# A two-layer decoder trunk on one core: MLP in a fixed order, weight sums by adding DMAs, norm gains and positions broadcast by TensorE

## The chip, the cores and the metric

The kernel runs on one core of a Trainium2 chip. The metric is the device time of one execution in microseconds. A core has a matrix engine (TensorE, PE in the profile, with its weight loads as PEld), a vector engine (VectorE, DVE), a scalar engine (ScalarE, ACT), GpSimd (POOL) and SyncE (SP), which here only starts DMAs. Each engine works through its own queue in order; semaphores order the engines among each other. TensorE writes to eight PSUM banks of 128 x 512 float32, and all other tiles lie in SBUF.

## What is computed

Two layers, sequence 512, model width 1024, everything in float32. The parts that matter here:

```python
for layer in range(DEPTH):                      # 2
    h = rms_norm(x, g_mix[layer])
    qkv = h @ w_in[layer]                       # 1024 x 3072, three head groups
    ...                                         # three kinds of attention, partial RoPE by positions
    x = x + mix @ w_out[layer]
    h2 = rms_norm(x, g_ffn[layer])
    u = h2 @ w_up[layer]                        # 1024 x 5632
    u = causal depthwise conv(u, width 3) + conv_b
    gate, val = split(u, 2)                     # 2 x 2816
    x = x + (silu(gate) * val) @ w_down[layer]  # 2816 x 1024
return rms_norm(x, g_final)
```

## The kernel before, in words

**Products.** Each float32 operand is split into a part that TensorE's fast float32 format holds (`whi`, a cast on ACT) and the rest (`wlo`, a subtraction on DVE); a product is three matmuls (hi x hi, hi x lo, lo x hi). The splits of the weights run through the whole program: SP loads a raw weight tile of 128 x 1024 (`raw`, five buffers), ACT casts it, DVE subtracts, TensorE uses the pair. The pairs have four buffers (`HL_BUFS`), so a split can start when the unit four before it has been used. One list of "units" gives their order; `use` takes the next units and splits some ahead (line 284).

**Opening.** x is loaded as four row tiles of two halves. For each tile ACT squares x (`square`, line 511), GpSimd multiplies x by the gain `gbc`, a tile of 128 x 512 that a DMA with step 0 fills with the same row in each partition (`load_g`, line 350), and DVE scales the product by the reciprocal root (`norm`, line 533); only the second half of the first tile is done by one DVE operation on x, `rstd` and `gbc`. TensorE transposes the result (`hT_of`, tiles `htp` and `hTh`, `hTl`), and the first projection (`qka`) starts with what is there. The positions come as a tile of 128 x 512 in the same way, on GpSimd's DMA queue (`rope_features`, line 425).

**MLP.** The up-projection runs in blocks: one block is 128 columns of `w_up`, 24 matmuls of 512 columns into one bank, gate (`upg`) and value (`upv`) in turn; f counts the pairs, 22 in all. A block's bank is read by the convolution (ACT scales it, DVE adds two shifted copies: `cg`, `cv`), then SiLU and the product of both on DVE.

The down-projection of f = 0 to 17 isn't done plainly. Three folds of six f take two rows of f (a pair: `g0`, `g1`) times a 2 x 2 block of `w_down` with seven products in place of eight (Winograd's form of Strassen's multiplication). It needs sums of the activations (`s`, on GpSimd, split into `ga` and `gs`) and sums of the weight blocks (`tt`, and one half of `raw`, on GpSimd too): four sums of 128 x 512 per pair.

```python
G.tensor_tensor(out=tt[:, 1], in0=r1[:, 1], in1=r0[:, 1], op=OP.subtract)
G.tensor_tensor(out=r0[:, 1], in0=r0[:, 1], in1=r0[:, 0], op=OP.subtract)
G.tensor_tensor(out=tt[:, 0], in0=r1[:, 1], in1=r0[:, 1], op=OP.subtract)
```

A product is six matmuls of 512 columns; a fold of three pairs has 21 products into four pairs of banks (`dx`, `dy`, `dz`, `dw`). When the first 12 are done, the banks are added up into x (`dc`, `du`, `dv`, `dt`), and the other nine go on in `dx`, `dw`, `dz`. The banks of `upg`, `dx` and `dy` share one set of four, and `upv`, `dz` and `dw` the other: a fold's banks are those of the last up-blocks. f = 18 to 21 are done plainly (`dn`).

**What sets the order.** The opening keeps program order on the engines. In the MLP a list scheduler sets the order of each queue by its own estimates and by priorities: weight splits have priority 300, and the convolutions of the pair before a fold (`held`, line 1073), which is needed only after the fold, have 400.

Of the kernel before, what the change touches and what calls it, by code (L numbers as in the profile page):

```python
# [18 lines left out]
NT = S // 128  # L19
# [13 lines left out]
HOLD_PRIO = 400  # L33
# [30 lines left out]
def kernel(  # L64
# [57 lines left out]
    SIDE = {"sc", "ptp", "pv", "ov", "stk", "htp", "cvp", "upv", "dz", "dw"}  # L122
# [54 lines left out]
    for l in range(DEPTH):  # L177
# [15 lines left out]
        for f0, n in FOLDS:  # L193
            add_up(l, f0 + 2, n)
            for f in range(f0, f0 + n, 2):
                units.append(("s1", w_down, l, f, None))
            for f in range(f0, f0 + n, 2):
                units.append(("s2", w_down, l, f, None))
# [6 lines left out]
    RAWS = {"t": 1, "f": 1, "s1": 2, "s2": 0}  # L205
    SLOTS = {"t": 1, "f": 1, "s1": 2, "s2": 2}
# [4 lines left out]
    def emit_dma(force=False):  # L211
# [15 lines left out]
        elif kind == "f":  # L227
            raw = raw_tile((128, KD, 128))
            nc.sync.dma_start(out=raw, in_=w[l, :, a:a + 128].rearrange("(k p) c -> p k c", p=128))
        elif kind == "s1":  # L230
            raw = [raw_tile() for _ in range(2)]
            for r, k in zip(raw, (a, a + 1)):
                nc.sync.dma_start(out=r, in_=w[l, k * 128:(k + 1) * 128, :].rearrange("p (c n) -> p c n", c=2))
# [6 lines left out]
            raw = r0, r1, tt  # L240
        else:
            raw = None
        raws[u] = raw
        return True

# [8 lines left out]
    def emit_split():  # L254
# [8 lines left out]
        with tc.high_priority(PRIO if u > 3 else 0):  # L263
# [6 lines left out]
            elif kind == "s1":  # L270
                r0, r1, tt = raw
                split[u] = hi_lo(r0), hi_lo(tt)
                kept[l, a] = r1, tt
                n_raw[0] -= 1
            else:

                r1, tt = kept.pop((l, a))
                G.tensor_tensor(out=tt[:, 1], in0=r1[:, 0], in1=tt[:, 0], op=OP.subtract)
                split[u] = hi_lo(r1), hi_lo(tt[:, 1:2], n=1)
                n_raw[0] -= 1  # L280
# [3 lines left out]
    def use(n=1, ahead=2):  # L284
# [3 lines left out]
        taken = sum(SLOTS[units[u][0]] for u in range(u0, u0 + n))  # L288
        while n_split[0] < u0 + n:
            emit_split()  # L290
        while n_split[0] < len(units):
            out = taken + sum(SLOTS[units[u][0]] for u in range(u0 + n, n_split[0] + 1))
            if out > (HL_BUFS if units[n_split[0]][0][0] == "s" else max(n, 1 + ahead)):
                break
# [61 lines left out]

    load_x(0)
    load_g(("mix", 0), g_mix[0])
# [14 lines left out]
    V.tensor_copy(identr, ident)  # L373
    eps_t = const.tile([128, 1], F, name="eps_t")
# [46 lines left out]

    cos_f = const.tile([128, 512], F, name="cos_f")
    sin_f = const.tile([128, 512], F, name="sin_f")

    def rope_features():
        pi = page("pos_i", I32)
        s = positions[0]
        nc.gpsimd.dma_start(out=pi, in_=bass.AP(tensor=s.tensor, offset=s.offset, ap=[[0, 128], [1, 512]]))
        ang, k, r = page("ang"), page("k"), page("r")
        V.tensor_copy(k, pi)  # L430
        V.tensor_scalar(out=ang, in0=k, scalar1=ropec[:, 0:1], scalar2=None, op0=OP.mult)
# [101 lines left out]
    def norm(t, g=None):  # L533
        r = rstd_of(t)
        for c in range(2):
            if g is None or c == 0:
# [387 lines left out]
    def mlp(l, nxt):  # L924
        cv = convs[l]

        def conv(banks, f):

            us = []
            for b, j, name in zip(banks, (f, NF + f), ("cg", "cv")):  # L930
                us.append((page(name), b, j))
            for u, b, j in us:
# [268 lines left out]
```

## Time and profile before

| | |
|---|---|
| median of 3 runs | 1271.05 us (1270.91 to 1273.56) |
| the profiled execution | 1272.82 us, its span 1271.0 us |
| TensorE busy | 1216.7 us (96%) |
| VectorE, ScalarE, GpSimd busy | 931.3, 669.6, 405.6 us |
| moved by DMA | 111.22 MB, 88 GB/s over the span |
| first matmul | 9.56 us after the start |

A row of the timeline gives the start, the duration, the engine, the operation with its tiles (out<-in), and in brackets the idle time before it with what ended it. Nearly all instructions bear line 99, which is a helper that records them; so they are told apart by the names of their tiles. In a row of groups, "x64: 1209/1226/2314" is the count with the shortest, median and longest time in ns, and "| 28.5, 1582 |" the sum in us and the mean in ns.

### The profile page before, as it was taken

Reading aid. Unit: us, or ns where it says so; the run is one execution under the profiler, and the core shown is the slowest. Engines: PE = TensorE matmul, PEld = TensorE weight load, DVE = VectorE, ACT = ScalarE, POOL = GpSimd, SP = SyncE. Lnnn points to the kernel's source line nnn. Section 1 sums busy time; section 2 is a strip of 40 time slices with the busy share of each in tenths; the row PEclk is TensorE's granted clock in tenths of the full one; section 3 lists DMA queues with packets and bytes.
Section 4 is the critical chain, followed back from the end, with each engine's and each line's share of the span. In section 5 each row is a group of like instructions: output and inputs, shape, how many; then the busy total and the mean of one; then the engine's idle time right before and its main releaser. Section 6 shows DMA issues by size and latency. Waiting matters only on the chain.

```text
span 1271.0 us, 16494 instructions
## 1 busy us (share of the span) xinstructions
PE 1216.7 (96%) x5888; PEld 988.9 (78%) x5888; DVE 931.3 (73%) x1619; ACT 669.6 (53%) x1224; POOL 405.6 (32%) x388
## 2 busy tenths in 40 slices
PE   6999999999989999999999999999999899999996
PEld 5877777789877877887888777787988788788785
DVE  6888878576678678678678677774766876776874
ACT  4766777544434444444457658773544344443444
POOL 3011435131254245154211123441124614525413
PEclk9999999999999999999999999999999999999999
DMA  6321212232314323324313121121332242242221
GB/s 225 103 83 51 67 51 69 68 97 86 100 55 127 101 66 105 115 80 125 99 42 117 51 83 50 67 70 50 117 100 84 83 133 83 67 133 83 67 83 67
DMA packets 142562, 111.22 MB, mean 88 GB/s; under 512 B 5386, under 2 KB 124208, under 8 KB 142480
## 3 DMA queue, kind: packets, MB, share of 16 engines
q1 hardware_dynamic: 142064, 109.47, 28.5%
q8 instruction: 46, 0.75, 0.2%
q0 software_dynamic: 272, 0.44, 0.1%
q14 instruction: 36, 0.29, 0.1%
q10 hardware_dynamic: 144, 0.26, 0.1%
HBM read 108.06 MB, written 2.10 MB: 87 GB/s over the span
## 4 chain that ended last, share of the span: by engine, by line
PE 49%; DVE 28%; POOL 9%; issue 7%; ACT 6%; DMA 2%; SPq 0%; POOLq 0%; ACTq 0%; DVEq 0%
DVE wlo L99 10%; PE upg L99 9%; PE upv L99 8%; PE op L99 7%; DVE cv L99 4%; PE qf L99 4%; POOL s L99 4%; ACT whi L99 3%; DVE p L99 3%; PE qka L99 3%; PE dn L99 3%; PE pv L99 3%; DVE cg L99 2%; PE up L99 2%; PE ptp L99 2%
## 5 line engine op out<-in xcount | busy, mean ns | idle before, releaser
L99 DVE TENSOR_TENSOR wlo<-raw,whi 128x1024 fp32r<-128x1024 f32 x196 | 271.1, 1385 | 112.5 <-ACT whi L99 111.5
L99 ACT CAST whi<-raw 128x1024 fp32r<-128x1024 f32 x196 | 203.9, 1047 | 137.4 <-PE dw L99 31.4
L99 POOL TENSOR_SCALAR p<-p,sm 128x512 f32<-128x512 f32 (+3 forms) x128 | 77.3, 612 | 240.8 <-DVE sm L99 149.5
L99 PE MATMUL upg<-hTh,wlo 128*128 128x512 f32 x320 | 125.0, 391 | 2.4 <-DVE wlo L99 2.4
L99 PE MATMUL upg<-hTh,whi 128*128 128x512 f32 x320 | 124.6, 389 | 0.0
L99 PE MATMUL upg<-hTl,whi 128*128 128x512 f32 x320 | 124.5, 389 | 0.0
L99 PE MATMUL upv<-hTh,whi 128*128 128x512 f32 x320 | 124.5, 389 | 0.0
L99 PE MATMUL upv<-hTl,whi 128*128 128x512 f32 x320 | 124.5, 389 | 0.0
L99 PE MATMUL upv<-hTh,wlo 128*128 128x512 f32 x320 | 124.5, 389 | 0.0
L99 POOL TENSOR_TENSOR hn<-x,gbc 128x512 f32<-128x512 f32 x39 | 53.2, 1375 | 174.9 <-ACT hn L99 168.1
L99 ACT ACTIVATE p<-p,sm 128x512 f32<-128x512 f32 (+3 forms) x160 | 89.2, 559 | 33.5 <-DVE sm L99 32.5
L99 POOL TENSOR_TENSOR s<-cv 128x256 f32<-128x256 f32 x36 | 34.6, 980 | 196.8 <-DVE cv L99 196.8
L99 POOL TENSOR_TENSOR tt<-raw 128x512 f32<-128x512 f32 x36 | 54.6, 1516 | 108.9 <-DMA raw<-in_w_down_dram 107.5
L99 ACT ACTIVATE cg<-cg 128x512 f32<-128x512 f32 x44 | 27.8, 632 | 115.2 <-DVE cg L99 115.0
L99 PEld LDWEIGHTS upg<-hTh,wlo 128*128 128x128 f32 x320 | 60.1, 188 | 16.4 <-DVE wlo L99 4.1
L99 PEld LDWEIGHTS upv<-hTh,wlo 128*128 128x128 f32 x320 | 60.1, 188 | 12.5
L99 PEld LDWEIGHTS upg<-hTl,whi 128*128 128x128 f32 x320 | 60.1, 188 | 12.4
L99 PEld LDWEIGHTS upv<-hTh,whi 128*128 128x128 f32 x320 | 60.1, 188 | 12.4
L99 PEld LDWEIGHTS upv<-hTl,whi 128*128 128x128 f32 x320 | 60.1, 188 | 12.4
L99 PEld LDWEIGHTS upg<-hTh,whi 128*128 128x128 f32 x320 | 60.1, 188 | 12.2
L99 DVE TENSOR_TENSOR wlo<-tt,whi 128x1024 fp32r<-128x1024 f32 (+1 forms) x36 | 49.8, 1382 | 25.1 <-ACT whi L99 24.8
L99 ACT CAST ga<-cv 128x256 fp32r<-128x256 f32 (+1 forms) x36 | 18.1, 514 | 87.9 <-DVE cv L99 87.9
(234 smaller groups left out, 3207.5 us busy)
## 6 DMA issues: line engine op xcount, KB each, us to landing
raw<-in_w_up_dram SPq DMA_DIRECT2D x88, 512.0 KB, 3.8
raw<-in_w_down_dram SPq DMA_DIRECT2D x44, 512.0 KB, 3.5
raw<-in_w_in_dram SPq DMA_DIRECT2D x40, 512.0 KB, 3.7
raw<-in_w_out_dram SPq DMA_DIRECT2D x16, 512.0 KB, 3.5
raw<-in_w_in_dram SPq DMA_DIRECT2D x16, 256.0 KB, 3.0
x<-in_x_dram SPq DMA_DIRECT2D x8, 256.0 KB, 7.1
out_dram<-hn SPq DMA_DIRECT2D x7, 256.0 KB, 2.1
gbc<-in_g_mix_dram SPq DMA_DIRECT2D x4, 256.0 KB, 5.6
```

What stands on the lines that cost most here:

```text
L99: i = f(*a, **k)
```

## The change

**Weight sums.** The units s1 and s2 of a pair become four units w1 to w4, and `FOLD_UNITS` gives their order in a fold. The weight sums are done by DMAs that add what they load to what lies in the tile (`accum_op=OP.add`). They can only be started from GpSimd's queue. `w1` is a load of the pair's first column half followed by one add into its second part; `tt` is loaded by SP and gets one add of 512 KB and one of 256 KB; when `w2` has been split from it, one more add of 256 KB makes `w4` of it. Some signs of the sums change with this, so that each weight sum is an addition.

**Fixed order.** From the third f of a layer's MLP to the end of its up-blocks each engine keeps program order, and the program writes that order out: a block's convolution is issued behind the next block's matmuls (`finish_conv`), splits run three units ahead, and work that can wait is put in a list (`later`) for the next block. In the fold, splits, the additions of the banks and the products stand in a given order; the held pair's operands are made behind the fold. The nine last products are in another order (`dx`, `dw`, `dz` per pair become 2, 4, 3 with the last two turned round).

**Opening.** The gain of layer 0's first norm is loaded as two rows of 1 x 512 from ACT's queue, and TensorE multiplies a column of ones by each row, which leaves the gain in all partitions of two PSUM banks (`over_rows`, tile `gb`). GpSimd's multiplications of the first norm go; DVE does each half in one operation. Positions are broadcast in the same way. The squares of the next tile are issued ahead of the transposes of this one.

```diff
+FOLD_UNITS = [("w1", 0), ("w1", 1), ("w2", 0), ("w2", 1), ("w1", 2), ("w2", 2),
+              ("w3", 0), ("w4", 0), ("w3", 1), ("w4", 1), ("w3", 2), ("w4", 2)]
...
-            r0, r1 = raw
-            tt = sb.tile([128, 2, 512], F, name="tt", tag="qkst", bufs=WIDE)
-            G.tensor_tensor(out=tt[:, 1], in0=r1[:, 1], in1=r0[:, 1], op=OP.subtract)
-            G.tensor_tensor(out=r0[:, 1], in0=r0[:, 1], in1=r0[:, 0], op=OP.subtract)
-            G.tensor_tensor(out=tt[:, 0], in0=r1[:, 1], in1=r0[:, 1], op=OP.subtract)
+            raw = raw_tile()
+            b = quarters(l, a)
+            nc.sync.dma_start(out=raw, in_=b[:, 0 if kind == "w1" else 1])
+            if kind == "w1":
+                adding.append((raw[:, 1], b[:, 0, 0]))
...
+    def add_now(dst, src):
+        tc.keep_in_program_order(nc.gpsimd.dma_start(out=dst, in_=src, accum_op=OP.add))
+
+    def add_loaded():
+        while adding:
+            add_now(*adding.popleft())
+
+    def sum_steps(l, a):
+        b = quarters(l, a)
+        tt = sb.tile([128, 2, 512], F, name="tt", tag="qkst", bufs=WIDE)
+        kept[l, a] = tt
+        tc.keep_in_program_order(nc.sync.dma_start(out=tt, in_=b[:, 0]))
+        return [lambda: add_now(tt, b[:, :, 1]), lambda: add_now(tt[:, 0], b[:, 1, 1])]
...
+            elif kind == "w2":
+                tt = kept[l, a]
+                split[u] = hi_lo(tt)
+                add_now(tt[:, 0], quarters(l, a)[:, 1, 0])
...
+    for c in range(2):
+        nc.scalar.dma_start(out=g_row[c], in_=g_mix[0:1, 512 * c:512 * c + 512])
     load_x(0)
-    load_g(("mix", 0), g_mix[0])
...
+    def over_rows(row):
+        b = bank("gb")
+        T.matmul(b, lhsT=ones, rhs=row, start=True, stop=True)
+        return b
...
+        def block(v, f, extra=None):
+            b = bank("upv" if v else "upg")
+            wh, wl = take()
+            for k in range(KD):
+                ah, al = act_h(k)
+                three_f(b, wh[:, k, :], wl[:, k, :], ah, al, k == 0, k == KD - 1)
+            done = finish_conv()
+            add_loaded()
+            while n_split[0] < min(n_used[0] + 3, len(units)):
+                emit_split()
...
         squares(0)
-        norm(0, gbc["mix", 0])
+        norm(0, gains)
         for n in range(NT):
             wts[n] = use(1, 0)
+            if n + 1 < NT:
+                squares(n + 1)
             hT_of(n)
             if n + 1 < NT:
-                squares(n + 1)
-                norm(n + 1)
+                norm(n + 1, gains)
```

How the queues stand now, at three places. First ACT's queue in the opening (`hn` is the squares' output, `whi` the cast of a weight tile, `hTh` the cast of the transposes), before:

```order
L99 ACT_TABLE_LOAD
L99 ACTIVATE hn,ss<-x_0_64 128x512
L99 ACTIVATE hn,ss<-x_1_65 128x512
L99 ACTIVATE rstd<-rstd,eps_t 128x1
L99 ACTIVATE rstd<-rstd 128x1
L99 CAST whi<-raw 128x1024
L99 CAST hTh<-htp 128x4x128 x2
L99 ACTIVATE hn,ss<-x_0_66 128x512
L99 ACTIVATE hn,ss<-x_1_67 128x512
```

With the change:

```order
L367 DMA g_row<-in_g_mix_dram 1x512 x2
L100 ACT_TABLE_LOAD
L100 ACTIVATE hn,ss<-x_0_64 128x512
L100 ACTIVATE hn,ss<-x_1_65 128x512
L100 ACTIVATE rstd<-rstd,eps_t 128x1
L100 ACTIVATE rstd<-rstd 128x1
L100 CAST whi<-raw 128x1024
L100 ACTIVATE hn,ss<-x_0_66 128x512
L100 ACTIVATE hn,ss<-x_1_67 128x512
L100 CAST hTh<-htp 128x4x128 x2
```

Two DMA starts stand at its head, and the squares of the second tile are ahead of the first `hTh`.

Second DVE's queue in the first fold of layer 0, behind the convolution of the last up-block (`wlo` are the weight splits, `du` and `dv` the additions of the banks, `ga` an operand of the held pair):

```order
L99 TENSOR_TENSOR wlo<-raw,whi 128x1024
L99 TENSOR_TENSOR wlo<-tt,whi 128x1024
L99 TENSOR_TENSOR wlo<-raw,whi 128x1024
L99 TENSOR_TENSOR wlo<-tt,whi 128x512
L99 TENSOR_TENSOR du<-dy,dc 128x512 x2
L99 TENSOR_TENSOR dv<-dw,du 128x512 x2
L99 TENSOR_TENSOR dv<-dz,dv 128x512
L99 TENSOR_TENSOR wlo<-raw,whi 128x1024
L99 TENSOR_TENSOR wlo<-tt,whi 128x512
L99 TENSOR_TENSOR dv<-dz,dv 128x512
L99 TENSOR_TENSOR wlo<-raw,whi 128x1024
L99 TENSOR_TENSOR ga<-cv,ga 128x256
```

With the change, from the same point on:

```order
L100 TENSOR_TENSOR wlo<-tt,whi 128x1024
L100 TENSOR_TENSOR wlo<-raw,whi 128x1024
L100 TENSOR_TENSOR wlo<-tt,whi 128x1024
L100 TENSOR_TENSOR wlo<-raw,whi 128x1024
L100 TENSOR_TENSOR wlo<-tt,whi 128x512
L100 TENSOR_TENSOR du<-dc,dy 128x512 x2
L100 TENSOR_TENSOR dv<-dw,du 128x512 x2
L100 TENSOR_TENSOR dv<-dz,dv 128x512 x2
L100 TENSOR_TENSOR wlo<-raw,whi 128x1024
L100 TENSOR_TENSOR wlo<-tt,whi 128x512
L100 TENSOR_TENSOR wlo<-raw,whi 128x1024
```

Five splits stand ahead of the first addition in place of four, no split parts the last two `dv`, and `ga` is gone from the fold; it stands behind it.

Third GpSimd's queue at the same fold, from activation sums (`s`) to the first use of `du`:

```order
L99 TENSOR_TENSOR s_3465<-cv 128x256
L99 TENSOR_TENSOR s_3466<-cv 128x256
L99 TENSOR_TENSOR s_3465<-s_3465,cv 128x256
L99 TENSOR_TENSOR s_3466<-cv,s_3465 128x256
L99 TENSOR_TENSOR tt<-raw 128x512
L99 TENSOR_TENSOR raw<-raw 128x512
L99 TENSOR_TENSOR tt<-raw 128x512
L99 TENSOR_TENSOR tt<-raw,tt 128x512 x3
L99 TENSOR_TENSOR dt<-du,x_0_68 128x512
```

With the change:

```order
L247 DMA tt<-in_w_down_dram 128x512
L247 DMA raw<-in_w_down_dram 128x512
L247 DMA tt<-in_w_down_dram 128x512
L247 DMA raw<-in_w_down_dram 128x512 x2
L100 TENSOR_TENSOR s_3518<-cv 128x256
L100 TENSOR_TENSOR s_3518<-s_3518,cv 128x256
L100 TENSOR_TENSOR s_3519<-cv 128x256
L100 TENSOR_TENSOR s_3519<-s_3518,cv 128x256
L247 DMA tt<-in_w_down_dram 128x512 x3
L100 TENSOR_TENSOR dt<-du,x_0_68 128x512
```

Where GpSimd added tiles it now starts DMAs, most of them ahead of the activation sums; the three starts ahead of `dt` are the adds that make `w4`.

More of the change, by code (lines that the diff above doesn't have):

```diff
@@ L287, in use @@
         n_used[0] += n
[L288 to L294, printed above, removed]
+        while n_split[0] < min(u0 + max(n, 1 + ahead), len(units)):
             emit_split()
@@ L1000, in product, with take, finish_conv @@
             now[0] += 1.36
-        def fold(pairs):
+        def take():
+            n_used[0] += 1
+            return split.pop(n_used[0] - 1)
+        last, cgs, gates, steps, later = [None], {}, {}, deque(), []
+        def finish_conv():
+            if last[0] is None:
+                return None
+            b, v, f = last[0]
+            last[0] = None
+            u = conv(b, NF * v + f, "cv" if v else "cg")
+            if v:
+                gates[f] = gated(cgs.pop(f), u)
+                return f
+            cgs[f] = u
+            later.insert(0, lambda: act(u, u, AF.Silu))
+            return None
@@ new lines, in block @@
+        def block(v, f, extra=None):
+            b = bank("upv" if v else "upg")
+            wh, wl = take()
+            for k in range(KD):
+                ah, al = act_h(k)
+                three_f(b, wh[:, k, :], wl[:, k, :], ah, al, k == 0, k == KD - 1)
+            now[0] += 5.4
+            done = finish_conv()
+            add_loaded()
+            while n_split[0] < min(n_used[0] + 3, len(units)):
+                emit_split()
+            work = later[:]
+            later.clear()
+            for w in work:
+                w()
+            if done is not None and extra:
+                extra(done)
+            if steps:
+                steps.popleft()()
+            last[0] = (b, v, f)
@@ L1044, in fold @@
             for t in range(2):
                 G.tensor_tensor(out=u4[t], in0=u2[t], in1=X[2 + t][0], op=OP.add)
[L1046 to L1051 removed]
+            p(5, 2)
+            for t in range(2):
+                tt(out=u3[t], in0=bw[t], in1=u2[t], op=OP.add)
@@ L1076, in mlp, with rest @@
-        gh, gl = quad("gh"), quad("gl")
+                tt(out=X[t][1], in0=u2[t], in1=bz[t], op=OP.subtract)
+            if hold is not None:
+                later.append(hold)
+            def rest():
+                for t in range(2):
+                    tt(out=X[2 + t][0], in0=bw[t], in1=u4[t], op=OP.add)
+            later.insert(0, rest)
+        bs = first_group()
+        for f in range(2):
+            cg, cvl = conv(bs[2 * f], f, "cg"), conv(bs[2 * f + 1], NF + f, "cv")
+            act(cg, cg, AF.Silu)
+            gates[f] = gated(cg, cvl)
@@ L1077, in mlp @@
+        while f < NF:
+            for v in range(2):
+                block(v, f, plain)
+            f += 1
+        plain(finish_conv())
+        in_order[0] = False
+        gh, gl = gh[0], gl[0]
         f0, n = PLAIN
-        for j in range(n):
-            g = held[j] if j < 2 else up_pair(f0 + j)
-            A.copy(gh[:, j, :], g)
-            V.tensor_tensor(out=gl[:, j, :], in0=g, in1=gh[:, j, :], op=OP.subtract)
         def act_g(k):
```

299 lines of the change are left out of this document (172 added, 127 removed).

## The prediction

> **What bounds the kernel now.** I read the page's busy shares first, then the busy time by stretch, then what TensorE waited for, then the order of time at two places.
>
> ```profile
> PE 1216.7 (96%) x5888; PEld 988.9 (78%) x5888; DVE 931.3 (73%) x1619; ACT 669.6 (53%) x1224; POOL 405.6 (32%) x388
> PE   6999999999989999999999999999999899999996
> 408.69 5.44 PE upv L99 x24
> ```
>
> TensorE is busy 96% of the span, so what can be won is its idle time plus the time in which it runs slowly after a pause. The forty slices place it: the first slice, the last, and two that read 8. The third row, from the chain, gives the rate where nothing is in the way: 24 matmuls of 512 columns in 5.44 us, 0.2267 us each. A fold of three pairs has 3 x 7 x 6 = 126 of them, so it needs 28.56 us; the twelve up-blocks between two folds need 65.28 us. Against that stands the table by stretches, cut where TensorE's first matmul of each fold and its first up matmul behind it start (columns: stretch, length, TensorE busy, clock, DMA share, GB/s):
>
> ```profile
> 302.28:367.56 65.28, 65.28 (x290) 1.00 0.30 89
> 367.56:402.20 34.64, 31.06 (x128) 0.95 0.27 76
> 402.20:468.36 66.16, 65.57 (x289) 1.00 0.35 104
> 468.36:500.64 32.28, 29.47 (x127) 1.00 0.28 82
> 500.64:566.81 66.17, 65.58 (x289) 1.00 0.35 104
> 566.81:597.26 30.45, 29.15 (x128) 1.00 0.33 94
> 986.17:1019.16 32.99, 29.44 (x128) 1.00 0.28 80
> 1085.32:1119.16 33.84, 30.87 (x128) 0.95 0.26 77
> 1185.32:1217.76 32.44, 29.48 (x128) 1.00 0.30 88
> ```
>
> Up-blocks run at the ideal. The six folds are 6.08, 3.72, 1.89, 4.43, 5.28 and 3.88 us longer than 28.56: **25.3 us**. The first up-stretch behind a fold is 0.88 us too long, four times with layer 1's two (1019.16 to 1085.32 and 1119.16 to 1185.32 are 66.16 each): **3.5 us**. Together 28.8 us, and this is what the change is about. Why it is lost, in the waits of TensorE in layer 0 and in the first fold:
>
> ```profile
> PE dw L99 <- DVE cv L99: 5.9, 3, 2.4
> PE dx L99 <- DVE wlo L99: 1.3, 2, 1.0
> PE upg L99 <- DVE wlo L99: 1.2, 2, 0.6
> 364.09 2.27 DVE L99 TENSOR_TENSOR wlo<-tt,whi 128x1024 fp32r<-128x1024 f32 x1 [1.70 <-ACT whi L99]
> 373.19 0.63 ACT L99 ACTIVATE cg<-cg 128x512 f32<-128x512 f32 x1 [6.84 <-DVE cg L99]
> 377.61 0.76 PE L99 MATMUL dw<-whi,gs 128*128 128x512 f32 x1 [2.40 <-DVE cv L99]
> L99 DVE TENSOR_TENSOR wlo<-raw,whi x64: 1209/1226/2314, 294.8 to 631.2; 128x1024 fp32r<-128x1024 f32 x64
> L99 POOL TENSOR_TENSOR tt<-raw 128x512 f32<-128x512 f32 x18 | 28.5, 1582 | 53.9 <-DMA raw<-in_w_down_dram 53.2
> L99 POOL TENSOR_TENSOR raw<-raw 128x512 f32<-128x512 f32 x9 | 15.1, 1672 | 0.7
> L99 POOL TENSOR_TENSOR tt<-raw,tt 128x512 f32<-128x512 f32 x9 | 13.4, 1494 | 23.8 <-DVE wlo L99 23.8
> ```
>
> The bank of dw still holds the last up-block, whose convolution DVE does late. DVE lags by then: a split (wlo) that takes 1.226 us in the median takes 2.27 at 364.09, beside POOL's weight sums, and it first waits 1.70 us for the cast of a tt that POOL must have summed; ACT's SiLU, ahead of further casts in its queue, then waits 6.84 us for the gate's convolution.
>
> **The change, part by part.** *Sums by adding DMAs.* Per fold POOL loses 12 of the 36 sums above, (28.5+15.1+13.4)/3 = 19 us, and gets 12 adding DMAs, nine of 256 KB and three of 512 KB. SP gets three loads of 512 KB more. No row shows an adding DMA; the nearest are POOL's plain one and loads of the same size, and the longest landing in the crowded opening:
>
> ```profile
> L428 POOL DMA_DIRECT2D pos_i<-in_positions_dram x1: 745/745/745, 29.4 to 29.4; - x1
> pos_i<-in_positions_dram POOLq DMA_DIRECT2D x1, 256.0 KB, 3.7
> raw<-in_w_down_dram SPq DMA_DIRECT2D x44, 512.0 KB, 3.5
> DMA to landing us min/median/max: 2.6/4.4/8.1
> 10.00:15.00 5.00, 4.63 (x14) 2.86 (x12) 3.58 (x6) 4.36 (x10) 2.15 (x2) 1.00 1.03 379
> ```
>
> Issue: 12 x 0.745 = 9 us of POOL in some 94, less than it gives up. Landing: between 2.6 us (the shortest row) and 8.1 (the longest); I take 5, since an add also reads what it adds to, and the rows of this size say 3.5 to 3.7. Traffic: a cycle of 98.4 us moves 66.16 x 104 + 32.28 x 82 = 9.5 MB; with 1.6 MB of loads and 3.9 MB of adds it is 15 MB in 94 us, 160 GB/s, and 200 if an add counts twice, under the 379 that the opening reached. Is an add ever awaited? The tightest is w4: the split of w2 ends before the fold's first product, the add follows, and w4's first product is the fourteenth, 13 x 1.36 = 17.7 us in; its cast stands in ACT's queue at about 11, with 1 us of slack behind it. So an add may take 12 us before it delays anything. The tt adds are two blocks apart (10.9 us), and w1's have four. At 5 us, and even at 8.1, it costs nothing; the cover is this slack.
>
> The Trainium skill gives a price here: the page "DMA: Bandwidth & Descriptors", section "Anatomy of one DMA — SWDGE (gpsimd) path", fits 2.0 us plus bytes over 436 GB/s, an estimate of 2.6 and 3.2 us for plain transfers, which changes no term; no run here shows it for adds.
>
> *Fixed order.* Put the fold's DVE queue into time, zero at its first product, with these rows and ACT's cast of 1.05 us (the first row is an up-stretch, busy time of TensorE, its weight loads, DVE, ACT and POOL):
>
> ```profile
> 302.28:367.56 65.28, 65.28 (x290) 54.05 (x289) 45.27 (x52) 29.55 (x41) 23.99 (x20) 1.00 0.30 89
> L99 DVE SCALAR_TENSOR_TENSOR cv<-upv,conv,cv 128x511 f32<-128x511 f32 (+1 forms) x40 | 29.8, 746 | 0.7
> L99 DVE TENSOR_TENSOR dv<-dw,du 128x512 f32<-128x512 f32 x6 | 4.1, 692 | 0.0
> L99 POOL TENSOR_TENSOR dt<-du,x 128x512 f32<-128x512 f32 x6 | 7.7, 1298 | 12.8 <-DVE du L99 12.8
> ```
>
> tt is summed long before, so I take it that DVE does not lag and only the last block's convolution is left at zero: ACT 0.77, two DVE operations of 0.75 and a product of 0.69 end at 3.2, and dw is first written at 4 x 1.36 = 5.4. So the 5.9 us of waits on cv go. The splits follow at 1.23 each, as buffers come free (four, one per unit): each is ready 3 us or more ahead, down to w3 of the second pair. That one waits for product twelve (16.3), its cast, and behind du and dv; dv ends at about 17.9, the split at 19.2, and its product starts at 20.4. Slack 1.2 us. There POOL's dt and du sums (1.3 us each) run, so a split can be stretched to 2.31: slack 0.1. The split for the first block behind the fold has its buffer at 24.5, ends at 27.2 and is wanted at 28.6. The fold's DVE total is 11.8 (splits) + 2.2 + 4.1 + 2.7 = 21 of 28.6 us. I leave 0.4 us of wait per fold: **+2.5**, ends 0 and 2.3 per fold (14). The held pair's operands, which stood in the middle of the fold, now come behind it, in up-blocks where DVE was busy 45.27 of 65.28 us.
>
> *Opening.* Rows in order of time, and the chain's gbc:
>
> ```profile
> 1.66 5.90 DMA gbc<-in_g_mix_dram
> 5.89 0.46 DVE L99 TENSOR_SCALAR rstd<-rstd 128x1 f32<-128x1 f32 x2
> 7.72 1.26 POOL L99 TENSOR_TENSOR hn<-x,gbc 128x512 f32<-128x512 f32 x1 [6.14 <-DMA gbc<-in_g_mix_dram]
> 9.42 0.75 DVE L99 SCALAR_TENSOR_TENSOR hn<-x,rstd,gbc 128x512 f32<-128x512 f32 x1
> 9.56 1.97 PE L99 MATMUL htp<-ident,hn 128*128 128x128 f32 x8 [9.56 <-DVE hn L99]
> 9.60 1.05 ACT L99 CAST whi<-raw 128x1024 fp32r<-128x1024 f32 x1 [3.94 <-DMA raw<-in_w_in_dram]
> 12.05 0.63 ACT L99 ACTIVATE hn<-x 128x512 f32<-128x512 f32 x1
> 16.52 1.97 PE L99 MATMUL htp<-ident,hn 128*128 128x128 f32 x8 [1.88 <-DVE hn L99]
> L99 PE MATMUL ov<-osq,bones x8: 591/592/595, 110.8 to 728.2; 128*128 128x512 f32 x8
> ```
>
> The first norm no longer waits for gbc and POOL: rstd is done at 6.35, one DVE operation of 0.75 on each half, first transpose at about 7.1 instead of 9.56. The two gain matmuls (0.59 as ov, double that cold) stand ahead of it; their rows must land by some 4 to 5 us. Weight and x loads move up past 512 KB of gbc, some 2 to 4 us; the second tile's squares now stand ahead of the first hTh, so they wait for x instead of 12.05. I get the second transposes 3 to 4 us earlier; from there TensorE is without gaps. **-3.5**, ends 0 (the loads set the pace anyway) and -5.3 (gbc's 4.0 behind x plus POOL's 1.26). Positions: one matmul of 0.6 lies in TensorE's queue: **+0.6**. The rest of layer 0's attention is the same work in a slightly other order: 0, plus or minus 2.
>
> Sum: -28.8 + 2.5 - 3.5 + 0.6 = -29.2. The profiled execution took 1272.8 us (span 1271.0, 1.8 around it); less 29.2 it is 1243.6. It lies 1.8 above the median of the runs, so the forecast is **1242 us**.
>
> **Rivals.** *The adds land late.* Place: w2 to w4 in each fold. From 12 us on, each microsecond of landing holds ACT's queue and so the fold. At 18.5 us, five times the row, 6.5 x 6 = 39 us come back against 29.2 won: about **1281**, slower; the sign turns at 12 + 29.2/6 = 17 us. For it: an add is in no row. Against: 3.7 us for the same size and queue, DMA share 0.35. The Trainium skill names a cause: "SBUF — State Buffer", the box on DVE blocking DMA: descriptors from GpSimd can't be written while DVE runs a 2-port operation. By its section "Who interferes with whom" tensor_tensor is not among the operations that do so, and the DVE rows quoted for the folds are TENSOR_TENSOR and SCALAR_TENSOR_TENSOR; no run here shows the effect, and it leaves the chance below as it is.
>
> *The fixed order makes waits of its own.* A queue that can't pass a late instruction: if the split behind dv is stretched each time, and the next ones with it, 2.3 us of each fold stay: -29.2 + 14 - 2.5, about **1254**. For it: slack 0.1 to 1.2 us, and 128x512 sums on POOL of 1.3 to 2.0 us beside it. Against: POOL has 19 us less to do.
>
> *The opening gives nothing*, because the loads pace it: 1242 + 3.5, about **1245**; the third slice of 5 us already runs at 379 GB/s.
>
> **How the numbers follow.** Forecast 0.63, with 1236 (ends -5.3, no wait left, attention -2) to 1248 as its own range; opening 0.12 at 1245; fixed order 0.17 at 1254; late adds 0.08, of which some 0.07 ends slower than 1271. The range is 1235 to 1256: it takes in all but the late adds and the tails. A measurement here can't tell less than 0.2% (2.5 us) from no change; faster 0.90, same 0.03, slower 0.07.
>
> **What would show it.** Right: the six fold stretches at 28.6 to 29.5 us, no wait of dw on cv, wlo's longest near 1.3 in the up-blocks, adds landing in under 8 us, first transposes at 7 to 8 us and the second near 13. Wrong: casts of tt waiting for a DMA (late adds), dx waiting for wlo in mid-fold (order), or transposes still near 16.5 (opening).

## Result, and the profile after

The changed kernel takes **1242.88 us** in the median of four runs (1242.29 to 1244.79), the kernel before 1270.98 us beside it (1269.91 to 1273.56): a ratio of 0.9779, with a 95% interval of 0.976 to 0.9797. The forecast was 1242.0 us, in a range of 1235 to 1256. Its profiled execution took 1242.3 us, with a span of 1240.5; the span before was 1271.0, so 30.5 us went between the two traces.

From the page of the changed kernel, the busy shares and the forty slices of TensorE:

```profile
PE 1211.2 (98%) x5894; PEld 988.5 (80%) x5894; DVE 901.1 (73%) x1620; ACT 675.8 (54%) x1224; POOL 364.7 (29%) x381
PE   8999899999999999999999999999999999999996
```

The two 8s of the folds, the twelfth and the 32nd slice, are gone; a new one stands in the fifth, 124 to 155 us. The table by stretches of the changed kernel, for layer 0 (the columns are length, then busy time of TensorE, of its weight loads, of DVE, ACT and POOL, then clock, DMA share and GB/s):

```profile
300.69:365.88 65.19, 65.19 (x289) 53.95 (x288) 45.53 (x56) 30.93 (x42) 22.10 (x22) 1.00 0.67 170
365.88:394.45 28.57, 28.57 (x128) 23.65 (x127) 22.98 (x23) 13.21 (x15) 16.26 (x12) 1.00 0.47 113
394.45:459.74 65.29, 65.29 (x290) 54.06 (x289) 44.84 (x56) 29.71 (x41) 18.52 (x19) 1.00 0.72 181
459.74:488.30 28.56, 28.56 (x128) 23.65 (x127) 22.99 (x23) 13.22 (x15) 16.28 (x12) 1.00 0.47 111
553.60:582.15 28.55, 28.55 (x128) 23.64 (x127) 22.66 (x24) 13.20 (x15) 11.75 (x8) 1.00 0.49 119
```

The three folds last 28.55 to 28.57 us, the ideal of 28.56; before they were 34.64, 32.28 and 30.45. From the first product of the first fold (365.9) to the end of the span it is now 874.6 us, before (367.6 to 1271.0) it was 903.4: 28.8 us, just the excess that the prediction had counted. The stretch ahead of the first fold got only 1.7 us shorter. What TensorE waited for in the whole program, four of its nine rows:

```profile
PE ptp L100 <- POOL p L100: 5.2, 11, 2.0
PE htp L100 <- DVE hn L100: 4.6, 6, 1.3
PE gb L100 <- DMA g_row<-in_g_mix_dram: 2.4, 1, 2.4
PE sc L100 <- ACT kh L100: 2.1, 1, 2.1
```

There is no row of an up-block or of a fold among them: the 5.9 us of dw behind cv are gone, and nothing stands in their place. Longer than before is the wait of sc for kh, which comes once, in layer 0's attention: 2.1 us, before 0.9. The casts of ACT that stand around the folds, first before, then after (busy time and mean; behind the bar the idle time of ACT just ahead of them):

```profile
L99 ACT ACTIVATE cg<-cg 128x512 f32<-128x512 f32 x44 | 27.8, 632 | 115.2 <-DVE cg L99 115.0
L99 ACT CAST gs<-s 128x512 fp32r<-128x512 f32 x36 | 22.3, 618 | 53.3 <-POOL s L99 53.3
```

```profile
L100 ACT ACTIVATE cg<-cg 128x512 f32<-128x512 f32 x44 | 27.8, 632 | 30.6 <-DVE cg L100 30.6
L100 ACT CAST gs<-s 128x512 fp32r<-128x512 f32 x36 | 20.8, 615 | 6.0 <-POOL s L100 6.0
```

ACT stood for 53.3 us in front of gs, the cast of a pair's sums, because POOL had not made them yet. The prediction did not read this row. It turned out to be one of the two lags that mattered (e6 and e7).

### The profile page after: what moved, and what is told of

Its sections match the earlier page's. It is cut to its first block, busy times and chain, and to the rows that moved or that the text cites. A ratio compares the mean times of both kernels' runs of the same rounds, so it can differ in the third digit from the quotient of the medians.

```text
span 1240.5 us, 16542 instructions
## 1 busy us (share of the span) xinstructions
PE 1211.2 (98%) x5894; PEld 988.5 (80%) x5894; DVE 901.1 (73%) x1620; ACT 675.8 (54%) x1224; POOL 364.7 (29%) x381
## 4 chain that ended last, share of the span: by engine, by line
PE 80%; DVE 12%; ACT 3%; issue 2%; POOL 1%; DMA 1%; SPq 0%; POOLq 0%; ACTq 0%; DVEq 0%
PE upg L100 18%; PE upv L100 18%; PE op L100 7%; PE dw L100 4%; PE dz L100 4%; PE dx L100 4%; PE qf L100 4%; DVE p L100 3%; PE qka L100 3%; PE dn L100 3%; PE up L100 3%; PE vab L100 3%; DVE wlo L100 3%; PE pv L100 2%; PE dy L100 2%
## 5 line engine op out<-in xcount | busy, mean ns | idle before, releaser
L100 DVE TENSOR_TENSOR wlo<-raw,whi 128x1024 fp32r<-128x1024 f32 x196 | 267.3, 1368 | 45.9 <-ACT whi L100 45.1
L247 POOL DMA_DIRECT2D tt<-in_w_down_dram x54 | 54.9, 1069 | 237.9 <-DVE wlo L100 124.8
L100 DVE SCALAR_TENSOR_TENSOR cv<-upv,conv,cv 128x511 f32<-128x511 f32 x80 | 59.9, 749 | 78.3 <-ACT cv L100 76.9
L100 DVE SCALAR_TENSOR_TENSOR cg<-upg,conv,cg 128x511 f32<-128x511 f32 x80 | 60.0, 749 | 50.4 <-ACT cg L100 49.0
L100 POOL TENSOR_TENSOR hn<-x,gbc 128x512 f32<-128x512 f32 x32 | 44.4, 1396 | 156.1 <-ACT hn L100 155.4
L100 ACT ACTIVATE cg<-upg,conv 128x512 f32<-128x512 f32 x40 | 31.2, 781 | 91.7 <-PE upg L100 91.7
L100 PEld LDWEIGHTS upv<-hTl,whi 128*128 128x128 f32 x320 | 60.1, 188 | 12.4
L100 PEld LDWEIGHTS upg<-hTl,whi 128*128 128x128 f32 x320 | 60.1, 188 | 12.3
L100 ACT ACTIVATE cv<-upv,conv 128x512 f32<-128x512 f32 x40 | 31.2, 780 | 68.1 <-PE upv L100 65.8
```

Source lines behind the costliest of these rows:

```text
L100: i = f(*a, **k)
L247: tc.keep_in_program_order(nc.gpsimd.dma_start(out=dst, in_=src, accum_op=OP.add))
```

## The experiments

All are edits of the changed kernel but e6 and e7, which are edits of the kernel before; the edits are shown shortened. Times are medians; where the times of two kernels lie closer than their intervals of some 2 us either way, the traces tell them apart by two places: the first matmul of vab (end of the opening) and the first product of the first fold.

**e1, the old opening.**

```
-    load_x(0)                      (weights as rows, two matmuls)
+    load_x(0)
+    load_g(("mix", 0), g_mix[0])   (128 rows, POOL's multiply)
     and squares, norm and positions as before
```

> The changed kernel with the opening and the positions as they were before: weights by a broadcast load, POOL's multiply, the second tile's squares behind the first transposes; folds and adding loads stay. TensorE's order up to the output projection of layer 0 is then instruction by instruction that of the kernel before. In the changed kernel vab began 4.5 us earlier than before (40.2 against 44.7) and the first fold 1.7 us earlier (365.9 against 367.6). Theory: those 1.7 us are the opening's whole net gain; 2.8 of the 4.5 were lost in layer 0's attention through the new order there. Then this kernel's first fold starts at 367.6, its folds last 28.6 each, and it takes 1242.9 + 1.7 = 1244.6. Rival: what was lost in attention comes from the new MLP code or from chance (a clock pause that falls anywhere), and the opening is worth its 4.5: 1247.4. Second rival: the opening is worth nothing, 1242.9.

Measured: 1243.61 us, vab at 44.1, first fold at 367.0, 322.9 us apart as in the kernel before; from there to the end 874.8. So undoing the whole opening costs 0.7 us by the medians, which lies inside the intervals, and 1.1 by the first fold. The theory holds in kind: the opening's gain is mostly lost again ahead of the first fold. It holds in size less well, since the opening itself varies from one execution to the next (table under e9).

**e2, the old positions alone.**

```
-        nc.gpsimd.dma_start(out=pi, in_=positions[0:1, :])
-        V.tensor_scalar(out=ang, in0=over_rows(pf), ...)
+        nc.gpsimd.dma_start(out=pi, in_=<128 rows of positions>)
+        V.tensor_scalar(out=ang, in0=k, ...)
```

> The changed kernel with the positions of the feature rope loaded into 128 rows again instead of one row and a matmul; norm weights stay rows. It takes one matmul (0.6 us) off TensorE and gives the scheduler a third order in layer 0's attention. Theory that the matmul is only a matmul: vab still begins near 40.2, the first fold 0.6 earlier at 365.3, 1242.3. Theory that the pause of 2.1 us before the first sc of the third head pair and the slow clock behind it belong to one particular order: they go or stay with the order, first fold anywhere from 363.1 (both gone, 1240.1) to 367 (1244).

Measured: 1243.84 us; but vab at 44.6, where both theories had 40.2, and first fold at 367.6. In attention sc waited 0.9 us for kh, as in the kernel before, and the stretch from vab to the first fold lasted 323.0 us, also as before. The first cast of a weight block and POOL's load of the positions in this kernel, in order of time:

```profile
1.59 0.72 POOL L446 DMA_DIRECT2D pos_i<-in_positions_dram  x1
10.40 1.04 ACT L100 CAST whi<-raw 128x1024 fp32r<-128x1024 f32 x1 [4.72 <-DMA raw<-in_w_in_dram]
16.78 1.94 PE L100 MATMUL htp<-ident,hn 128*128 128x128 f32 x8 [0.64 <-DVE hn L100]
```

With the norm weights as rows, POOL has nothing to do early, and its 256 KB of positions start at 1.59 us (in the kernel before at 29.39), among the first weight loads: these land after 8.7 to 9.8 us, in the changed kernel after 6.1 to 7.2. The opening's gain is gone with that. So the positions' row earns what the weights' rows could not keep alone, and the order that comes with its matmul then gives most of it back in attention. Neither theory had the first half.

**e3, no fixed order in the MLP.**

```
-        in_order[0] = True
         f = 2
```

> The changed kernel with the fixed order left off in the MLP: adding loads stay, the scheduler may move the other instructions of DVE, ACT, POOL and TensorE by its own priorities. TensorE's order comes out the same, DVE's and ACT's do not. The change won 28.8 us in the folds and the stretch behind each. Theory that the order wins most: splits again stand behind convolutions and the other way round, folds last 31 to 33 us, and 15 to 25 us come back: 1258 to 1268. Theory that taking the sums off POOL wins most: folds near 29, 1243 to 1250.

Measured: 1245.64 us (ratio 0.9796, 0.9781 to 0.981), the first fold in 28.99 us (its first product at 366.34, the first up matmul behind it at 395.33), 877.5 from first product to end against 874.6. Of the 28.8 us, 2.9 come back: five folds last 29.0 us, the third 29.3, and the up-stretches behind them stay at the ideal. ACT waits 29.2 us ahead of gs there, where it waited 53.3 before. The theory that the order wins most falls.

**e4, POOL's sums in place of the adds, order kept.**

```
-        nc.gpsimd.dma_start(out=dst, in_=src, accum_op=OP.add)
+        nc.gpsimd.tensor_tensor(out=dst, in0=dst, in1=src, op=OP.add)
```

> The changed kernel with every adding load replaced by a sum on POOL (a plain load of a quarter into a tile of its own where the operand is not in SBUF yet), in the same fixed order: 15 sums of 128x512 per fold, by the 1.58 us of such a sum before some 24 us of POOL beside 22 and 16 us of other work in a cycle of 94. DVE's and ACT's orders stay those of the changed kernel. Theory that the order wins most: sums have blocks of lead, DVE's splits are stretched in places but the slack of the order takes it, 1243 to 1248. Theory that POOL's sums slow DVE down and make tt late: splits of 1.8 to 2.3 us beside them, casts of tt waiting for POOL, two to four us per fold, 1255 to 1268.

Measured: 1245.09 us (0.9797, 0.9781 to 0.9813), and 874.9 from first product to end. The first up-stretch and fold:

```profile
301.60:366.87 65.27, 65.27 (x291) 54.02 (x289) 51.19 (x56) 30.86 (x42) 33.50 (x28) 1.00 0.43 133
366.87:395.44 28.57, 28.57 (x128) 23.66 (x127) 22.98 (x22) 13.21 (x15) 18.01 (x13) 1.00 0.31 93
```

POOL is busy 33.5 us where it was 22.1, DVE 51.2 where it was 45.5, and TensorE does not notice. ACT waits 13.5 us ahead of gs. So it is not the adding DMAs by themselves that win. The sums do slow DVE down, but the theory that this costs two to four us a fold falls. Each half, taken away by itself, leaves the gain standing.

**e5, both undone.** The edits of e3 and e4 together.

> The changed kernel with both undone at once: POOL makes the weight sums and the scheduler is free to order the MLP. What stays of the change is how the MLP's code is cut (convolution of a block written behind the next block, operands of the held pair behind the fold, splits three units ahead, other product order). Undone singly, neither gave anything back in the folds beyond 3 us. Theory that either cover is enough, and the loss of the kernel before came from both lags together (ACT's queue held by casts that wait for POOL, DVE's splits stretched beside POOL): 15 to 28 us come back, 1258 to 1271. Theory that the new cut of the code wins it whatever engine sums and whatever order: 1244 to 1250.

Measured: 1262.27 us (1257.70 to 1267.77), 899.0 us from first product to end in its profile, which is that of its slowest execution, where the kernel before has 903.4. TensorE's first row of waits in this kernel:

```profile
PE dw L100 <- DVE cv L100: 13.4, 6, 3.4
```

And its group of gs casts, with ACT's idle time ahead of them behind the bar:

```profile
L100 ACT CAST gs<-s 128x512 fp32r<-128x512 f32 x36 | 21.7, 615 | 47.8 <-POOL s L100 47.8
```

The wait of dw for cv is back, and with it the wait ahead of gs. So the first theory holds: either half is enough, and the loss needs both lags at once. The new cut of the code by itself wins some 9 us by the medians and 4.4 by the two traces. By the traces it wins them behind the folds and not in them: the six folds of e5 (34.28, 29.58, 33.63, 31.30, 33.76 and 32.88 us) are together 24.1 us longer than the ideal, before 25.3, while the up-stretches behind them are at 65.28.

**e6, the kernel before without POOL's weight sums.**

```
-            G.tensor_tensor(out=tt..., ...)     (three sums, a fourth for w4)
+            nc.sync.dma_start(out=tt, in_=<a row block of w_down>)
```

> The kernel before without POOL's twelve weight sums per fold: the tile tt is loaded with a row block of the weights instead (one more 512 KB load on SP per pair), so the MLP's output is not the reference's; all other instructions stay, in an order the scheduler makes anew. If POOL's weight sums are what made DVE and ACT late, the folds fall to 28.6 to 29.5 us each and it takes 1243 to 1250. If the old cut of the code is enough to make them late, 1262 to 1271.

Measured: 1251.16 us (0.984, 0.9825 to 0.9854), 881.1 us from first product to end: between both theories, nearer to the first. 22.3 of the 28.8 us go with the sums, although ACT still waits 47.7 us ahead of gs. The six folds last 29.0 us each, as the first theory has it. What stays is mostly the four up-stretches behind folds, which are 0.88 us too long as before (66.16 the first), with upg waiting for wlo.

**e7, the kernel before with two casts moved.**

```
             A.copy(dst[:, j:j + n], src)        (for gs only:)
+            behind(that copy, last A.activation of the next value block)
```

The subtraction on DVE that follows each of these casts moves with it, and the scheduler places a few splits and ga casts around them anew.

> The kernel before with one thing moved: the two casts of a pair's sums (gs) stand behind the cast-and-bias of the next value block in ACT's queue, where they stood ahead of a split's cast and waited for POOL (53.3 us in all before, the last of them 3.06 us ahead of the first fold, with DVE idle for 2.67 right behind). TensorE's order stays. If that wait at the head of ACT's queue is what DVE's lag at the folds starts from, most of the 28.8 us goes: 1245 to 1255. If the lag comes from the stretched splits and from SiLU ahead of casts, little changes: 1266 to 1272.

Measured: **1245.89 us** (0.9799, 0.9785 to 0.9814), with all of POOL's weight sums, the free order and the old opening in it; 877.3 us from first product to end. Its group of gs casts:

```profile
L99 ACT CAST gs<-s 128x512 fp32r<-128x512 f32 x36 | 20.4, 615 | 0.0
```

Its first fold and the stretch behind it, cut where TensorE's first product and its first up matmul behind the fold start (columns as above):

```profile
366.60:395.60 29.00, 28.86 (x127) 23.57 (x126) 23.31 (x25) 14.52 (x18) 17.56 (x12) 1.00 0.33 97
395.60:460.88 65.28, 65.28 (x289) 54.05 (x288) 49.59 (x54) 27.96 (x38) 26.48 (x19) 1.00 0.33 102
```

No cast of gs waits any more, each of the six folds lasts 29.0 us, 0.44 above the ideal, and the stretches behind them are at it. This one edit takes 26.1 of the 28.8 us; the rest is the 0.44 us six times. In the kernel before, the rows of ACT and DVE ahead of the first fold (first product at 367.56) read like this, with the start of a later convolution in the last:

```profile
357.51 0.62 ACT L99 CAST gs<-s 128x512 fp32r<-128x512 f32 x1 [3.06 <-POOL s L99]
358.04 1.05 ACT L99 CAST whi<-raw 128x1024 fp32r<-128x1024 f32 x1
358.16 0.69 DVE L99 TENSOR_TENSOR gs<-s,gs 128x512 fp32r<-128x512 f32 x1 [2.67 <-ACT gs L99]
360.86 1.53 DVE L99 SCALAR_TENSOR_TENSOR cg<-upg,conv,cg 128x511 f32<-128x511 f32 x2
```

The same convolution in e7 (first product at 366.60):

```profile
353.58 1.52 DVE L99 SCALAR_TENSOR_TENSOR cg<-upg,conv,cg 128x511 f32<-128x511 f32 x2
```

The split's cast (whi) stands behind the gs cast, which waits for POOL, and DVE idles for 2.67 us. DVE starts this convolution 6.7 us ahead of the fold's first product, in e7 13.0 us ahead. Of these 6.3 us the idle time and the two subtractions of gs (0.7 us each), which e7 moves, make 4.0; the rest stood already in front of them.

**e8, w4's add twice over.**

```
+                for _ in range(2):
                     add_now(tt[:, 0], quarters(l, a)[:, 1, 0])
```

> The changed kernel with the add that makes w4 done twice over, one behind the landing of the other (the block is added twice, so the MLP's output is not the reference's). In the first fold of the changed kernel these adds start at 364.55, 370.67 and 374.19 and the casts that read them at 376.96, 382.40 and 386.48: 12 us each. Theory of 12 us of cover: two landings of 4.1 to 5 us in a row end by 374, 380 and 385, just ahead of the casts; POOL's sum dt starts up to 1.5 us later; nothing or up to 1 us per fold: 1243 to 1249. Rival, that the cover is shorter than the rows say because the casts' place in ACT's queue or POOL's own sums bind first: 3 us and more per fold, 1260 and more.

Measured: 1283.69 us (1.0087, 1.0062 to 1.0111), 41 us more than the changed kernel. Seven us a fold: the first theory falls by far. Where it goes, in rows of POOL, DVE, ACT and TensorE in order of time, from this kernel's first fold (first product at 364.90):

```profile
383.16 0.86 POOL L247 DMA_DIRECT2D tt<-in_w_down_dram  x1 [6.22 <-DMA tt<-in_w_down_dram]
383.72 2.87 POOL L100 TENSOR_TENSOR dt<-du,x 128x512 f32<-128x512 f32 x2
385.23 8.07 DVE L100 TENSOR_TENSOR wlo<-raw,whi 128x1024 fp32r<-128x1024 f32 x1 [1.38 <-ACT whi L100]
388.91 0.62 ACT L100 CAST whi<-tt 128x512 fp32r<-128x512 f32 x1 [3.72 <-DMA tt<-in_w_down_dram]
393.35 0.50 PE L100 MATMUL dx<-wlo,ga 128*128 128x512 f32 x1 [3.58 <-DVE wlo L100]
```

The last block does land too late for its cast, by 3.72 us; but it is not what TensorE waits for. A split of DVE took 8.07 us in place of 1.22, while POOL ran its six sums (dt, du, x<-x,dv) with no gap, and 18.8 us into the fold, not 14.0 as in the changed kernel. Every fold has one such split, 8.07 to 9.31 us long. TensorE waits 28.0 us in all for them (dw 20.5, dx 7.5), and the rest of the 41 goes mainly at the slow clock behind these waits: 0.71 in the 5 us from 395 on in the first fold.

**e11, POOL's sums late, adds single.**

```
-            dt and du on POOL as soon as du is there
+            dt and du on POOL behind x<-x,dv
```

> The changed kernel, adds single as they were, with POOL's four sums dt and du moved behind its two sums x<-x,dv: the six of a fold then run in one go from the moment dv is there (some 383 in the first fold, where dt began at 379.85), as they did from 383.72 where w4's add was doubled. The orders of TensorE, DVE and ACT are those of the changed kernel. There one split of a fold took 8 to 9.3 us beside these six sums of POOL, and 41 us were lost. Theory that DVE's split stands still while POOL's sums run without a gap, and that the late adds only moved the sums: a split of 8 us and more in each fold here too, 1275 to 1290. Rival, that the doubled adds themselves (landing late, or their traffic) made it: splits stay at 2.3 at the most, 1243 to 1246.

Measured: 1245.8 us (0.979, 0.9775 to 0.9804), no stall in the folds. POOL's sums do start at 383.55 and run without a gap, yet DVE's splits beside them take 1.8 to 2.3 us as in the changed kernel. Rows of POOL and DVE in order of time:

```profile
383.55 3.53 POOL L100 TENSOR_TENSOR x<-x,dv 128x512 f32<-128x512 f32 x2 [7.43 <-DVE dv L100]
387.05 3.98 POOL L100 TENSOR_TENSOR dt<-du,x 128x512 f32<-128x512 f32 x2
387.56 2.32 DVE L100 TENSOR_TENSOR wlo<-raw,whi 128x1024 fp32r<-128x1024 f32 x1
```

The theory of the gapless sums falls: here the two engines take turns (POOL needs 3.5 to 4.0 us for two sums, in e8 2.87).

**e12, two of a fold's three adds doubled.**

> The changed kernel with w4's add doubled for two of the three pairs of a fold (so the MLP's output is not the reference's) and single for the last. POOL is then done with its adds by 377 in the first fold, ahead of dt's 379.85, while the two pairs' blocks land 5 to 6 us later than in the changed kernel, still ahead of their casts (376.96 and 382.40). Theory that adds landing late cost nothing inside the 12 us, and POOL's sums at their old place cost nothing either: 1243 to 1245. Rival, that doubled adds cost by themselves: two thirds of the 41 us, 1270.

Measured: 1242.97 us (0.9768, 0.9752 to 0.9785), no stall in the folds. The second pair's first add started at 373.47; its block, added twice, was there for the cast at 385.29, which waited 0.38 us for it:

```profile
385.29 0.62 ACT L100 CAST whi<-tt 128x512 fp32r<-128x512 f32 x1 [0.38 <-DMA tt<-in_w_down_dram]
```

That is 11.8 us of cover, used to its end, at no cost; and a doubled add costs nothing by itself. What e8 has that neither e11 nor e12 has is an add issued directly ahead of the sums (383.16 and 383.72 above; in e12 dt waited another 1.27 us for DVE). Whether it is that, and why, stays open: no run tried it alone.

**e9 and e10, one place in attention.**

```
+    behind(first matmul of each of the 8 scores, 15th (e10: 18th) matmul of the next kf)
```

> The changed kernel with one place of layer 0's attention reordered: the eight score matmuls of the third head pair stand behind 15 matmuls of the next pair's kf where they stood behind 7 (nothing else is moved by hand). In the changed kernel TensorE stood still for 2.11 us there, waiting for the cast kh, and the granted clock read 0.69 in the 5 us behind it; from the first vab to the first fold it took 325.7 us, against 322.9 in the order of the kernel before. Theory that this one pause costs the 2.8 us: eight matmuls (1.8 us) fill it, no slow clock follows, first fold at 363.1 to 363.9, 1240 to 1241. Rival: DVE, busy 4.9 of 5 us there, sets the pace of this stretch, and the pause turns up at the next transposes: first fold still near 365.9, 1243.

> The same with 18 matmuls ahead of the scores. By the row (2.11 us, nine to ten matmuls of 0.2267) 18 instead of 7 cover the whole wait, but the scores and the softmax behind them start 0.4 us later than they could. Theory of the one pause: as with 15, 1240 to 1241, a tenth or two either way. Rival of DVE's pace: 1243 or a little more.

The place in the changed kernel, TensorE's rows in order of time:

```profile
129.28 1.02 PE L100 MATMUL sc<-kh,qh 128*128 128x512 f32 x3 [2.11 <-ACT kh L100]
131.49 0.63 PE L100 MATMUL kf<-hTl,whi 128*128 128x512 f32 x1
```

And the stretches around it (TensorE, its weight loads, DVE, ACT, POOL, then the clock):

```profile
125.00:130.00 5.00, 2.89 (x13) 2.15 (x12) 4.91 (x9) 3.53 (x6) 0.90 (x1) 0.97 0.31 92
130.00:135.00 5.00, 5.00 (x20) 4.30 (x19) 4.16 (x13) 3.92 (x11) 1.96 (x2) 0.69 0.39 108
```

Measured: e9 1241.83 us (0.9764, 0.9751 to 0.9777), e10 1243.03 (0.9773, 0.9759 to 0.9786). In both the wait for kh is gone or short, and a new one stands a little behind it. TensorE's waits in attention, first e9, then e10:

```profile
PE sc L100 <- DVE sm L100: 1.7, 1, 1.7
```

```profile
PE sc L100 <- DVE sm L100: 1.9, 1, 1.9
```

In e9 the clock stays at 1.00, and from vab to the first fold it takes 323.9 us, 1.8 of the 2.8 us back. In e10 the clock falls to 0.88 in the stretch from 130 to 135 us, where the wait is, and 0.78 in the next, and it takes 325.9, nothing back. So the rival is right about the pause, which turns up elsewhere while DVE sets the pace. That e9's order saves the slow clock isn't shown: e8 has the order of the changed kernel there and the same wait of 2.11 us, and its clock stays at 1.00 (rows in the last section). Against e8's 324.9 us e9 wins 1.0. e9 is the fastest of all by its median, 1 us below the changed kernel; their intervals overlap, so that it is faster isn't shown.

The two places in all kernels that share an order in attention (us of the span; the last column is their difference):

| Kernels | first vab | first fold | between |
|---|---|---|---|
| old opening: before, e1, e7 | 44.7, 44.1, 43.7 | 367.6, 367.0, 366.6 | 322.9 each |
| old opening: e6 | 44.1 | 368.5 | 324.4 |
| e2 (weights as rows, old positions) | 44.6 | 367.6 | 323.0 |
| new opening: after, e3, e4, e5 | 40.2, 40.6, 41.2, 41.4 | 365.9, 366.3, 366.9, 367.0 | 325.7, 325.7, 325.7, 325.6 |
| new opening: e8, e11, e12 | 40.0, 41.3, 41.8 | 364.9, 366.9, 368.7 | 324.9, 325.6, 326.9 |

The order of TensorE's work between the two places is the same in all rows with the old positions, and the same in all rows with the new opening. What differs inside such a group goes mostly with the clock in layer 0's attention. Without a slow stretch the old order takes 322.9 to 323.0 us and the new one 324.9 (e8); with one they take 324.4 (e6) and 325.6 to 325.7; with two the new order takes 326.9 (e12). So the new order costs 2.0 us when neither has a slow stretch, and 2.8 in the two kernels that were compared.

The new opening puts vab at 40.9 in the mean of seven, the old one at 44.2 in the mean of four: 3.2 us earlier. The first fold starts at 366.7 in the mean of the seven and at 367.4 in that of the four. The opening and the positions together are worth some 0.8 us by these means, less than the first folds of one group scatter (364.9 to 368.7), so a gain isn't shown.

## Why the prediction was right, step by step

*What bounds the kernel.* Right as a place and as a sum: the six folds and the stretches behind them held 28.8 us, and all of it went. **Only half of the cause was seen.** The prediction took the weight sums on POOL for what made DVE late, through splits stretched beside them and a tt summed late. The other half is the cast gs, which waited for POOL's activation sums at the head of ACT's queue, with a split's cast behind it. The loss needs both: without the weight sums 22.3 us of it go though gs still waits (e6), and without the wait of gs 26.1 go though every sum is there (e7); in both the folds are at 29.0 us. The change touches both lags twice over, since the adds take the weight sums off POOL and the fixed order writes gs a block later. This fits with either half of it keeping the gain (e3, e4) and both undone losing it (e5).

*Adding DMAs at no cost.* Right. Their rows on the page of the changed kernel (KB, median us to landing):

```profile
tt<-in_w_down_dram POOLq DMA_DIRECT2D x18, 512.0 KB, 7.7
tt<-in_w_down_dram POOLq DMA_DIRECT2D x36, 256.0 KB, 4.5
raw<-in_w_down_dram POOLq DMA_DIRECT2D x18, 256.0 KB, 4.8
```

And the group of their issues on POOL (busy time and mean):

```profile
L247 POOL DMA_DIRECT2D tt<-in_w_down_dram x54 | 54.9, 1069 | 237.9 <-DVE wlo L100 124.8
```

The landing of 5 us holds for 256 KB; 512 KB took 7.7, near the upper end. The issue was 1.07 us, not 0.745. The traffic of a cycle is (181 x 65.29 + 111 x 28.56) / 93.85 = 160 GB/s, as estimated. The cover of 12 us from w2 to w4 can be read off in the first fold, add against cast, rows of POOL and ACT in order of time:

```profile
364.55 0.88 POOL L247 DMA_DIRECT2D tt<-in_w_down_dram  x1 [12.88 <-DVE wlo L100]
374.19 0.88 POOL L247 DMA_DIRECT2D tt<-in_w_down_dram  x1 [2.67 <-DVE wlo L100]
376.96 0.62 ACT L100 CAST whi<-tt 128x512 fp32r<-128x512 f32 x1 [1.67 <-PE dy L100]
386.48 0.62 ACT L100 CAST whi<-tt 128x512 fp32r<-128x512 f32 x1 [0.30 <-PE dz L100]
```

It is 376.96 - 364.55 = 12.4 us for the first pair and 12.3 for the last, and e12 used 11.8 of it for nothing. What the prediction missed is that POOL waits in its own queue where two adds follow one another, so a late add holds POOL's sums up before it holds a cast (e8).

*Fixed order, +2.5.* This term was too large: the residue is 0. The place it named is the right one. The split of w3 behind dv was put at 17.9 to 19.2 us in the fold; it ran from 383.01 to 384.74, that is 17.1 to 18.9, and its product begins 20.4 in: 1.5 us of slack, where 1.2 was counted and 0.1 feared. It was stretched to 1.73 us beside POOL's sums; the 2.31 feared came two splits later (at 386.36), where there was room.

*Opening, -3.5.* Right in size: -4.5 between the two profiled executions, -3.2 in the mean of all. The first transpose came at 7.47 us (7.1 was forecast) and the second at 14.14 (near 13). The reason was told by halves: that the positions' row keeps 256 KB out of the first 10 us was not in it, and without that nothing is won (e2).

*Positions and attention, +0.6 and 0 plus or minus 2.* **This is the term that was too small**: it cost 2.8 us in the profiled execution. The broadcast of the positions was put at one matmul of 0.6 us; TensorE ran it as two, 1.1 us together:

```profile
L100 PE MATMUL gb<-pos_f,ones x2: 587/640/692, 55.1 to 55.7; 1*128 1x512 f32 x2
```

From vab to the first fold TensorE is busy 316.8 us in the changed kernel and 314.4 in the kernel before; of these 2.4 us the broadcast is 1.1, and the other 1.3 are the slow clock behind the pause. Idle time grew by only 0.4 us, from 8.4 to 8.9. In e8, which has no slow clock there, TensorE is busy 315.5 us and idle 9.4. That this term and the 2.5 of the fixed order that did not come nearly cancel is luck; with it the sum stayed right: forecast -28.8 + 2.5 - 3.5 + 0.6 = -29.2; measured between the two traces -28.8 + 0 - 4.5 + 2.8 = -30.5.

*The rivals.* No add was awaited by the folds, and the fixed order made no wait. "The opening gives nothing" is nearly what happened in net, not because loads set the pace but because attention gave it back.

## What to carry to other kernels

Where an engine with an in-order queue stands next to the path, look at what the head of its queue waits for, and not only at what is slow: moving the two casts of a pair that waited up to 3 us for a third engine, with the subtraction behind each, won 25 of the 28 us that the whole change of some 470 lines won. When two halves of a change are each said to win the time, undo them singly and together; a gain that survives either undoing hangs on lags that only count together. And one instruction put on TensorE in the middle of a stretch that a scheduler orders can cost more in all (2.0 to 2.8 us here) than by itself (1.1).

## What the runs showed of the hardware that was not expected

A pause of TensorE of about two us was followed by a slow clock in some executions and not in others. After the 2.11 us at 127 in the changed kernel the matmuls that start 0.2267 us apart elsewhere started 0.43 apart (131.49, 131.92 and 132.34, 0.63 us each in place of 0.39), and the granted clock from 130 to 135 us was 0.69. In e8 the same matmul waited equally long at the same place, and the clock stayed at 1.00:

```profile
129.09 0.79 PE L100 MATMUL sc<-kh,qh 128*128 128x512 f32 x3 [2.11 <-ACT kh L100]
130.00:135.00 5.00, 4.75 (x25) 3.87 (x24) 4.88 (x19) 4.04 (x12) 2.33 (x3) 1.00 0.37 108
```

The other way round, a wait of 1.85 us that left the clock at 1.00 in the kernel before was followed by 0.77 and 0.89 in the stretches from 160 and 165 us of e6, which has the same order there; first the kernel before, then e6:

```profile
162.87 1.31 PE L99 MATMUL ptp<-ident,p 128*128 128x128 f32 x10 [1.85 <-POOL p L99]
```

```profile
162.25 2.04 PE L99 MATMUL ptp<-ident,p 128*128 128x128 f32 x10 [1.85 <-POOL p L99]
```

So the length of one pause doesn't decide it in the range seen here, and what does is open. The Trainium skill, page "TensorE: Matmul & The Clock Gate", section "Part 1: The HAM clock gate (the "warmup" mystery)", has the clock halved after an idle window of some 3.4 us; the halving agrees, the length does not: here less than that was enough at times.

DVE and POOL mostly take turns: a split of 1.22 us took 1.73 to 2.32 beside POOL's sums. But in e8 one split a fold took 8.07 to 9.31, about as long as POOL's six sums together. The Trainium skill, page "SBUF — State Buffer", section "Who interferes with whom", says that a DVE operation with two SBUF inputs contends with a GpSimd operation that reads SBUF, and that the contention is an exclusive lock. The stretching agrees: at 0.5 to 1.1 us it is less than one sum of POOL (1.29 us in the mean of dt), so each time the split may have stood still for one. Why it stood through six of them in e8 is open.

The same opening code put the first vab between 40.0 and 41.8 us in nine profiled executions (e9 and e10 at 41.3 and 40.7): about as much as the whole 1.7 us by which the first fold moved.
